# Moving the weight sums of a group behind the low parts beside them, and the weight casts behind the bank copies, in a two-layer decoder trunk

## The chip, the cores and the metric

The kernel runs on one core of a Trainium2 chip. The metric is device time of one execution in microseconds (us), the median of several executions. The engines are named as in the profile: PE is TensorE (PEld its weight loads), DVE is VectorE, ACT is ScalarE, POOL is GpSimd, SP is SyncE, which issues most DMA transfers.

## The reference

Two layers over 256 tokens with a model width of 2048, batch 1, everything in float32:

```
h = x
layer 0: hn = rms_norm(h);  proj = hn @ w_in   (2048 x 6144, split x, y, q, f, v, g)
         RG-LRU on x, y and HGRN2 on q, f, v, g;  h += concat(lru, hgrn) @ w_out
         h += square(relu(rms_norm(h) @ w1)) @ w2      (2048 x 8192, 8192 x 2048)
layer 1: hn = rms_norm(h);  q, k, v = hn @ w_qkv;  rotary, dilated window attention (16 heads)
         h += attn @ w_o
         h += square(relu(rms_norm(h) @ w1)) @ w2
out = rms_norm(h)
```

Nearly all the work is products of a 256-row activation with large weights that are each used once.

## The kernel before

**Precision in two parts.** A weight tile of 128 x 2048 floats (1 MB) is brought in and split: ACT casts it to a high part, tile `hi`, and DVE subtracts that from the tile and leaves the low part, tile `lo`. Activations are held in two parts too (`bufa`, `bufb`, `formx`, `formh`). A product is then three products: high by high, low by high, and high by low. `Weights.split` issues the cast and the subtraction. There are three buffers each for the incoming tile (`raw`), for `hi` and for `lo`.

**Groups with seven products instead of eight.** Most products (half of `w_out` and `w_o`, all of `w_qkv`, `w1` and `w2`) run in groups. A group treats two blocks of 128 tokens, two interleaved halves of the depth and two column blocks of 512 as a 2 x 2 by 2 x 2 product and does it with seven products of blocks. `blocks` runs one group, `combine` prepares its weights. There are 40 groups in the program, 32 of them in the two MLPs. In the table `ORDERS` a group's steps are

```
a  t1  d  t2  n  c  n  t3  n  t4  n        (a few groups exchange the last two, or the two plain tiles)
```

`a`, `d`, `c` are weight tiles as they come. `t1` uses a sum of two tiles, `s = a + t1` (DVE, the first sum). `t2` uses `s + c` (DVE, the second sum, `add("s", "s", "c")`). `t3` uses a tile to which a POOL-issued DMA adds another tile on its way in (tile `t`), and `t4` uses `s` after such an accumulating DMA. The steps `n` are plain tiles used for both token blocks and take twice the time on PE.

**Banks.** The group accumulates in four PSUM banks, `alpha`, `beta`, `gamma`, `delta`. Step `a` fills `beta`, and a copy on ACT carries it into `gamma` before step `d` adds to `gamma`. Step `t1` fills `alpha`, and a second copy carries it into `delta`, which the `n` steps need. `t2` goes on in `beta`. The copies are issued by `seed`. In the profile the first copy reads `COPY p<-pd`, `p<-po` or `p<-pt`, the second `COPY p<-p`. Step `d` on PE reads `p<-hi,bufa` or `p<-hi,bufb`, step `t1` is `p<-hi,formx` or `formh` and `p<-lo,...`, step `t2` the same with `pd`, `po` or `pt` on the left.

**What sets the order.** All instructions of one engine run in the order of its queue. That order is made when the program is built: a scheduler picks the next ready instruction by priority, where weights (`stream`) come 150 places and evacuations and seeds (`urgent`) 400 places early. `after(ins, names)` adds an edge that only orders two instructions. Weight tiles are fetched two steps ahead: `unit` of step `a` fetches `d` (and with it `c` and the second sum), `unit` of `t1` fetches `t2`, and so on.

In the kernel before, the second sum is issued ahead of the split of `d`, except in two groups: the one of `w2` that starts at tile 56 (`LATE_SUM`) and the one of `w1` that starts at tile 64. The first sum has an edge to the low part of the tile before it in one group of `w_qkv` only.

Of the kernel before, what the change touches and what calls it, by code (L numbers as in the profile page):

```python
# [41 lines left out]
def trunk_kernel(ctx, tc, head, x, xtok, xback, cols, tab, masks, pos, fin, w_in, w_gate, w_out, w_qkv, w_o, w1, w2, out):  # L42
# [15 lines left out]
    class InOrder:  # L58
        on = False

        def __init__(self, engine):
            self.engine, self.last = engine, []
# [12 lines left out]
    V, A, T = InOrder(nc.vector), InOrder(nc.scalar), nc.tensor  # L75
# [27 lines left out]
    made = {}  # L103
    loads, casts = [], []
# [26 lines left out]
                    plan2(src, layer * 64 + q * 16 + 4 * n)  # L131
    at = [0, 0]

    class Weights:
        def __init__(self, raw, step=2048):
            self.raw = raw
            self.hi = whi.tile([P, 2048], F32R, name="hi")
            self.lo = wlo.tile([P, 2048], F32R, name="lo")
            for at in range(0, 2048, step) if step else ():
                self.split(at, step)  # L140

        def split(self, at, n, w=None):
            h, l = self.part(at, n)
            if w is None:
                w = self.raw[:, at:at + n]
            else:
                h, l = (t.rearrange("p (k c) -> p k c", c=512) for t in (h, l))
            casts[:] = [after(A.copy(h, w), [])]

            def low():  # L150
                i = V.tensor_tensor(l, w, h.bitcast(F32), OP.subtract)
                self.ins = getattr(i, "ins", i)
            if InOrder.on and ticks:
                lows.append(low)
            else:
                low()
# [20 lines left out]
    def combine(u, src, i, what, i0):  # L177
        def load(name, j, home=wraw):
            held[name] = home.tile([P, 2048], F32, name="raw" if home is wraw else name)
            nc.sync.dma_start(held[name], src[j])  # L180

        def add(to, x, y):
            return V.tensor_tensor(held[to], held[x], held[y], OP.add)

        if what == "a":
            load("t1", i0 + 4, both)
            load("a", i)
            held["s"] = both.tile([P, 2048], F32, name="s")
            i = add("s", "a", "t1")
            if src is w_qkv and i0 == 8:  # L190
                after(i, [made[u - 1].ins.name])
        elif what in ("n", "d"):
            load(what, i)
        def make(step=2048):
            made[u] = Weights(held[{"t1": "s", "t2": "s", "t3": "t1", "t4": "s"}.get(what, what)], step)

        ahead = units[u + 1][2:3] if u + 1 < len(units) else ()
        if ahead == ("t2",):
            load("c", i0 + 5)
            nc.gpsimd.dma_start(held["t1"], src[i0 + 5], accum_op=OP.add)  # L200
            if (src is w2 and i0 == LATE_SUM) or (src is w1 and i0 == 64):
                make()
                after(add("s", "s", "c"), [made[u].ins.name])
                return
            add("s", "s", "c")
        make()
        if what == "c":
            nc.gpsimd.dma_start(held["s"], src[i0 + 1], accum_op=OP.add)
# [49 lines left out]
    def mm(*args, **kw):  # L258
        chain[:] = [after(T.matmul(*args, **kw), chain)]  # L259
# [6 lines left out]
    def flush(due=None):  # L266
        todo = later[:due]
        del later[:due]
        for f in todo:
            f()  # L270
# [8 lines left out]
    def after(ins, names):  # L279
        ins = getattr(ins, "ins", ins)  # L280
        for n in names:
            tc.add_manual_dep(ins, n, NOSYNC, reason="order on one engine")
        return ins.name
# [384 lines left out]
    def lru_in(n, half):  # L668
        b0 = 4 * n + 2 * half
        p = turned("po", [done[f"x{n}"]] * 2, (2 * half, 2 * half + 1), back=True)  # L670
        for i in range(2):
            b = b0 + i
            A.activation(xc[:, b], p[:, i], AF.Identity, bias=col("conv_b", b), scale=col("conv_w", 24 + b))
            for t in range(3):
                V.scalar_tensor_tensor(xc[:, b, 3 - t:], p[:, i, :S - 3 + t], col("conv_w", 8 * t + b),
                                       xc[:, b, 3 - t:], op0=OP.mult, op1=OP.add)
            yield
        split_to(bufb[:, b0:b0 + 2], xc[:, b0:b0 + 2])
        yield
# [36 lines left out]
    def lru_gelu(n):  # L716
        y = done[f"y{n}"]
        q = outs[f"y{n}"] = vgs.tile([P, 2, 512], F32, name="tk", bufs=7)
        for j in range(2):
            A.activation(q[:, j], y[:, j], AF.Square, scale=math.sqrt(0.044715))  # L720
            V.scalar_tensor_tensor(q[:, j], q[:, j], 1.0, y[:, j], op0=OP.add, op1=OP.mult)
            lut(q[:, j], q[:, j], AF.Sigmoid, scale=2.0 * math.sqrt(2.0 / math.pi))
            V.tensor_tensor(y[:, j], y[:, j], q[:, j], OP.mult)
            yield
# [9 lines left out]
    def reload():  # L734
        for j in range(2):
# [3 lines left out]
                 c=[lru_in(0, 0), lru_in(0, 1), lru_in(1, 0), lru_in(1, 1),  # L739
                    lru_gelu(0), lru_out(0, 0), lru_out(0, 1), lru_gelu(1), lru_out(1, 0), lru_out(1, 1)],  # L740
# [91 lines left out]
    def blocks(src, i0, n0, mov, forms, events, final):  # L832
        plain = lambda j, k: (mov[:, k, j * P:j * P + P], mov[:, k, S + j * P:S + j * P + P])
        form = lambda f, k: (forms[:, k, 0, f * P:f * P + P], forms[:, k, 1, f * P:f * P + P])
        side = {"a": lambda i: plain(0, 2 * i), "d": lambda i: plain(0, 2 * i + 1), "t4": lambda i: plain(1, 2 * i + 1),
                "t1": lambda i: form(3, i), "t2": lambda i: form(0, i), "t3": lambda i: form(1, i),
                "c": lambda i: form(2, i)}
        alpha, delta, gamma = (pmm.tile([P, 512], F32, name="p") for _ in range(3))
        beta = psc.tile([P, 512], F32, name=("pd" if i0 % 16 else "pt") if src is w_qkv else "po" if n0 else "pd", bufs=1)
        bank = {"a": beta, "t1": alpha, "t2": beta, "c": alpha, "t3": beta, "d": gamma, "t4": beta}  # L840
        sums = {(0, 0): gamma, (0, 1): beta, (1, 0): alpha, (1, 1): delta}
        opened = []

        def times(bank, w, get, at=0, m=512, out_=None):
            out_ = bank if out_ is None else out_
            parts = [(i, k, 0) for i in range(4) for k in range(2)] + [(i, 0, 1) for i in range(4)]
            for n, (i, k, low) in enumerate(parts):
                mm(out_, get(i)[k], w.part(i * 512 + at, m)[low], start=not any(b is bank for b in opened),
                   stop=n == 11, skip_group_check=True)
                opened.append(bank)  # L850

        def seed(to, bank):
            with urgent():
                A.copy(to, bank)
            opened.append(to)

        plains, did = [0, 0], []
        for what, u in order_of(src, i0 + 4 * n0):
            w = unit(src, None if u is None else i0 + 4 * n0 + u)
            due = len(later)  # L860
            did.append(what)
            if what == "t4" and plains[0] == 2:
                times(beta, w, side[what], 0, S, beta[:, :S])
                final(0, 1, beta)
                rest = psc.tile([P, 512], F32, name="pt", bufs=1)
                times(rest, w, side[what], S, S, rest[:, :S])
                events["rest"](rest[:, :S])
            elif what != "n":
                times(bank[what], w, side[what])
                if what == "a":  # L870
                    seed(gamma, beta)
                elif what == "t1":
                    seed(delta, alpha)
                elif what in events:
                    events[what](bank[what])
                if what == "t2":
                    flush(due)
            else:
                n, g = divmod(u, 4)
                plains[n] += 1  # L880
                for j in range(2):
                    times(sums[n, j], w, lambda i, j=j, g=g: plain(j, 4 * g + i))
                    if plains[n] == 2 and (n, j, "t4" in did) != (0, 1, False):
                        final(n, j, sums[n, j])
                flush(due)
            turn_some()
            for f in steps.pop(0) if steps else ():
                f()
# [283 lines left out]
    with urgent():  # L1172
        for j in range(2):
# [13 lines left out]
            h = tmp.tile([P, 2], F32, name="nr2", bufs=2)[:, :1]  # L1187
# [38 lines left out]


LAST = 2
LATE_SUM = 56
PRIO = 150  # L1230
URGENT = 400
ORDER = "v0 x0 x1 q0 G0 f0 q1 f1 G1 v1 g0 y0 g1 y1"
# [116 lines left out]
```

## Time and profile before

| | |
|---|---|
| median of 3 executions | 2151.09 us (2147.95, 2151.09, 2156.37) |
| profiled execution | 2153.47 us, span of its instructions 2151.7 us |
| mean granted TensorE clock | 0.996 |
| PE busy | 2116.8 us, 98% of the span, 9712 matmuls |
| DVE busy | 1725.2 us, 80% |
| ACT busy | 1359.9 us, 63% |
| DMA | 500.15 MB, mean 232 GB/s |

The time is that of the executions, the span is the stretch between first and last instruction in the one profiled execution, 1.8 us shorter. PE is the engine that is nearly always at work, so the table is read as follows: any gap on PE is time, and work on the other engines matters only where PE waits for it. In a timeline row the columns are start and duration in us, engine, line, operation, output and inputs, shape and count; brackets at the end give the idle time of that engine just before the row, and what released it. Almost all rows stand on L68 (a helper that issues for ACT and DVE) or L259 (the helper of matmuls), so tiles tell them apart.

### The profile page before, as it was taken

The numbers are of one execution on the slowest core, as the hardware profiler recorded it, in microseconds if no ns is written. First come the engines' busy times: TensorE is split into PE (matmuls) and PEld (weight loads), VectorE is DVE, ScalarE is ACT, GpSimd is POOL, SyncE is SP. The second block draws the span as 40 slices with busy tenths as digits, with TensorE's granted clock in tenths as the row PEclk, the third lists the DMA queues.
The fourth block names the chain that finished last, engine by engine and source line by source line (L and its number), as shares of the span: only waits on it lengthen the run. The fifth ranks groups of instructions, "written<-read, shape, count | busy, mean of one in ns | idle before, by whom it ended". The sixth has DMA issues, their size and how long they took to land.

```text
span 2151.7 us, 24879 instructions
## 1 busy us (share of the span) xinstructions
PE 2116.8 (98%) x9712; PEld 1753.8 (82%) x9712; DVE 1725.2 (80%) x1640; ACT 1359.9 (63%) x1438; POOL 72.3 (3%) x89
## 2 busy tenths in 40 slices
PE   9999999999999999999999999999999999999998
PEld 8888888878878888878888888887888888788787
DVE  7686969887778888788887788788878877877787
ACT  7577556665566566576666666566755755655664
POOL 0000000000000000000000000000000000000000
PEclk9999999999999999999999999999999999999999
DMA  8444457777877787778777767477877787778775
GB/s 341 176 176 157 170 218 237 237 223 236 266 251 217 249 260 253 248 228 268 234 242 239 232 225 231 160 215 235 247 271 233 240 253 262 217 235 266 249 246 157
DMA packets 70453, 500.15 MB, mean 232 GB/s; under 512 B 7872, under 2 KB 8128, under 8 KB 10560
## 3 DMA queue, kind: packets, MB, share of 16 engines
q1 hardware_dynamic: 58176, 413.29, 49.1%
q0 software_dynamic: 11872, 84.94, 21.6%
q8 instruction: 76, 1.25, 0.2%
q10 hardware_dynamic: 288, 0.34, 0.0%
q14 instruction: 41, 0.34, 0.0%
HBM read 496.44 MB, written 2.10 MB: 232 GB/s over the span
## 4 chain that ended last, share of the span: by engine, by line
PE 78%; DMA 8%; DVE 6%; ACT 4%; issue 3%; DVEq 0%; ACTq 0%
PE p L259 54%; PE po L259 9%; PE pd L259 8%; DMA raw<-in_w 7%; DVE s L68 3%; ACT hi L68 3%; DVE lo L68 3%; PE pt L259 3%; PE pl L262 2%; PE pl L259 1%; ACT p L68 1%; DMA t<-in_w 0%; DMA t<-in_w_qkv 0%; DVE xall L68 0%; DVE y L68 0%
## 5 line engine op out<-in xcount | busy, mean ns | idle before, releaser
L68 DVE TENSOR_TENSOR lo<-raw,hi 128x2048 fp32r<-128x2048 f32 (+1 forms) x364 | 785.8, 2170 | 115.9 <-ACT hi L68 114.9
L68 ACT CAST hi<-raw 128x2048 fp32r<-128x2048 f32 (+1 forms) x364 | 659.3, 1817 | 284.6 <-PE pd L259 79.7
L259 PE MATMUL p<-hi,bufa 128*128 128x512 f32 x2000 | 511.8, 398 | 19.2 <-ACT p L68 19.2
L259 PEld LDWEIGHTS p<-hi,bufa 128*128 128x128 f32 x2000 | 374.7, 190 | 101.1 <-ACT p L68 25.7
L68 DVE TENSOR_TENSOR lo<-s,hi 128x2048 fp32r<-128x2048 f32 x120 | 274.8, 2290 | 65.8 <-ACT hi L68 63.9
L259 PE MATMUL p<-hi,bufb 128*128 128x512 f32 x1264 | 319.9, 392 | 5.8 <-ACT p L68 5.8
L68 ACT CAST hi<-s 128x2048 fp32r<-128x2048 f32 x120 | 229.3, 1911 | 150.3 <-PE p L259 78.4
L259 PEld LDWEIGHTS p<-hi,bufb 128*128 128x128 f32 x1264 | 235.2, 188 | 57.0 <-ACT p L68 9.0
L259 PE MATMUL p<-lo,bufa 128*128 128x512 f32 x1000 | 269.8, 390 | 0.0
L259 PEld LDWEIGHTS p<-lo,bufa 128*128 128x128 f32 x1000 | 188.0, 188 | 40.0 <-DVE lo L68 0.3
L259 PE MATMUL p<-lo,bufb 128*128 128x512 f32 x632 | 172.9, 389 | 0.0
L68 DVE TENSOR_TENSOR s<-s,raw 128x2048 f32<-128x2048 f32 x40 | 91.6, 2291 | 82.5 <-DMA raw<-in_w 75.5
L68 DVE TENSOR_TENSOR lo<-t,hi 128x2048 fp32r<-128x2048 f32 x40 | 91.6, 2291 | 63.2 <-ACT hi L68 63.2
L259 PEld LDWEIGHTS p<-lo,bufb 128*128 128x128 f32 x632 | 118.7, 188 | 24.8
L68 ACT CAST hi<-t 128x2048 fp32r<-128x2048 f32 x40 | 76.5, 1913 | 91.7 <-PE p L259 85.8
L68 DVE TENSOR_TENSOR s<-raw,t 128x2048 f32<-128x2048 f32 x40 | 91.3, 2283 | 0.4 <-DMA raw<-in_w_o 0.4
L259 PE MATMUL pd<-hi,bufa 128*128 128x512 f32 x352 | 88.5, 393 | 0.6 <-DVE y L68 0.5
L259 PE MATMUL p<-hi,formx 128*128 128x512 f32 x352 | 87.6, 391 | 0.0
L259 PE MATMUL po<-hi,bufb 128*128 128x512 f32 (+1 forms) x320 | 78.6, 388 | 0.4 <-DVE xall L68 0.4
L68 ACT ACTIVATE y<-y 128x512 f32<-128x512 f32 x96 | 60.6, 631 | 26.1 <-DVE y L68 23.8
L259 PEld LDWEIGHTS pd<-hi,bufa 128*128 128x128 f32 x352 | 65.0, 188 | 14.3 <-DVE y L68 1.4
L259 PEld LDWEIGHTS p<-hi,formx 128*128 128x128 f32 x352 | 65.6, 188 | 13.4
(314 smaller groups left out, 2529.8 us busy)
## 6 DMA issues: line engine op xcount, KB each, us to landing
raw<-in_w SPq DMA_DIRECT2D x224, 1024.0 KB, 8.4
raw<-in_w_in SPq DMA_DIRECT2D x45, 1024.0 KB, 4.8
raw<-in_w_qkv SPq DMA_DIRECT2D x42, 1024.0 KB, 7.8
t<-in_w SPq DMA_DIRECT2D x32, 1024.0 KB, 6.4
t<-in_w POOLq DMA_DIRECT2D x32, 1024.0 KB, 9.3
s<-in_w POOLq DMA_DIRECT2D x32, 1024.0 KB, 9.2
raw<-in_w_out SPq DMA_DIRECT2D x15, 1024.0 KB, 4.8
raw<-in_w_o SPq DMA_DIRECT2D x15, 1024.0 KB, 4.9
```

The source lines that it names most:

```text
L68: i = call(*args, **kw)
L259: chain[:] = [after(T.matmul(*args, **kw), chain)]
L262: chain[:] = [after(T.transpose(out_, in_, ident), chain)]
```

## The change

Three things are done to the order; no arithmetic and no transfer is added or removed.

- The second sum `s + c` is issued behind the split of `d` in every group, with an edge to the low part of `d`.
- The first sum `s = a + t1` gets an edge to the low part of the tile before it, in every group whose preceding tile has one.
- The cast of a weight tile gets an edge to the bank copy that was issued last (`seeds`).

```diff
+    seeds = []
+
     class Weights:
         def __init__(self, raw, step=2048):
-            self.raw = raw
+            self.raw, self.ins = raw, None
...
-            casts[:] = [after(A.copy(h, w), [])]
+            casts[:] = [after(A.copy(h, w), seeds)]
...
             held["s"] = both.tile([P, 2048], F32, name="s")
             i = add("s", "a", "t1")
-            if src is w_qkv and i0 == 8:
+            if u - 1 in made and made[u - 1].ins:
                 after(i, [made[u - 1].ins.name])
...
             nc.gpsimd.dma_start(held["t1"], src[i0 + 5], accum_op=OP.add)
-            if (src is w2 and i0 == LATE_SUM) or (src is w1 and i0 == 64):
-                make()
-                after(add("s", "s", "c"), [made[u].ins.name])
-                return
-            add("s", "s", "c")
+            make()
+            after(add("s", "s", "c"), [made[u].ins.name])
+            return
         make()
...
         def seed(to, bank):
             with urgent():
-                A.copy(to, bank)
+                seeds[:] = [after(A.copy(to, bank), [])]
             opened.append(to)
```

Three places show what that does to the queues. The first is DVE in a group of `w1` in layer 0 (its two sums; `t_4401` is the second operand of its first sum, the `xall` rows are results of the group before it). Lines with - stand in the kernel before, lines with + in the changed one.

```order
 L68 TENSOR_TENSOR lo<-s,hi 128x2048
 L68 SCALAR_TENSOR_TENSOR xall<-po,r2n,xall 128x512
+L68 TENSOR_TENSOR lo<-raw,hi 128x2048
 L68 TENSOR_TENSOR s<-raw,t_4401 128x2048
-L68 TENSOR_TENSOR lo<-raw,hi 128x2048 x2
+L68 TENSOR_TENSOR lo<-raw,hi 128x2048
 L68 TENSOR_TENSOR lo<-s,hi 128x2048
 L68 SCALAR_TENSOR_TENSOR xall<-p,nm_3307,xall 128x512
-L68 TENSOR_TENSOR s<-s,raw 128x2048
 L68 SCALAR_TENSOR_TENSOR xall<-po,nm_3307,xall 128x512
 L68 TENSOR_TENSOR lo<-raw,hi 128x2048
+L68 TENSOR_TENSOR s<-s,raw 128x2048
```

The first sum now has the low part of the preceding tile ahead of it, and the second sum (`s<-s,raw`) has moved behind the low part of `d`.

The second place is ACT in the same group, around its two bank copies (`hi<-s` is the cast for `t2`).

```order
 L68 CAST hi<-s 128x2048
 L68 CAST hi<-raw 128x2048
-L68 CAST hi<-s 128x2048
-L68 COPY p<-pd 128x512
-L68 CAST hi<-raw 128x2048
-L68 COPY p<-p 128x512
-L68 CAST hi<-raw 128x2048 x2
+L68 COPY p<-pd 128x512
+L68 COPY p<-p 128x512
+L68 CAST hi<-s 128x2048
+L68 CAST hi<-raw 128x2048 x3
```

Both copies now stand ahead of the cast for `t2` and of the one for the plain tile behind it.

The third place is ACT in the group behind that one (`y_...` and `formh` are results of the `w1` group before it on their way to `w2`).

```order
-L68 CAST hi<-raw 128x2048
+L68 CAST formh<-y_4613 128x2x2x128
+L68 CAST hi<-raw 128x2048
+L68 CAST formh<-y_4532 128x2x2x128
 L68 ACTIVATE y_4740<-pd 128x512
-L68 CAST formh<-y_4613 128x2x2x128
+L68 COPY p<-po 128x512
 L68 ACTIVATE y_4740<-y_4740 128x512
-L68 CAST hi<-s 128x2048
-L68 COPY p<-po 128x512
-L68 CAST formh<-y_4532 128x2x2x128
```

Here the two `formh` casts have moved ahead as well, to both sides of the cast of `d`, and the copy stands between two activations.

The pattern of the second place, both copies and then the cast for `t2`, holds in 37 of the 40 groups. Two of them had it before, the ones whose second sum was already late. In the three attention groups of `w_qkv` that are left the cast for `t2` stays between the two copies. The order on PE does not change; on POOL the transfers keep their order, except that two loads of the final gains pass one accumulating transfer near the end.

More of the change, by code (lines that the diff above doesn't have):

```diff
@@ L1228 @@
 LAST = 2
-LATE_SUM = 56
 PRIO = 150
```

## The prediction

> **What bounds the kernel now.** I read the busy shares of the page first, then the waits of PE, then the timeline around the largest of them.
>
> ```profile
> PE 2116.8 (98%) x9712; PEld 1753.8 (82%) x9712; DVE 1725.2 (80%) x1640; ACT 1359.9 (63%) x1438; POOL 72.3 (3%) x89
> ...
> PE p L259 <- ACT p L68: 24.9, 23, 3.0
> ...
> DVE s L68 <- DMA raw<-in_w: 75.5, 29, 4.0
> ```
>
> PE is at work for 98% of the span, so only its gaps can be won or lost. Nearly all that the profile names of them is one wait, 24.9 us in 23 pieces: step `d`, which adds to a bank that ACT has to fill by the first copy. The third row is what stands behind it: DVE waits 29 times for the tile `c` that its second sum needs. One `w1` group of layer 0 shows how the two hang together:
>
> ```profile
> 569.68 1.91 ACT L68 CAST hi<-raw 128x2048 fp32r<-128x2048 f32 x1 [3.48 <-PE po L259]
> ...
> 571.55 2.29 DVE L68 TENSOR_TENSOR s<-s,raw 128x2048 f32<-128x2048 f32 x1 [2.36 <-DMA raw<-in_w]
> ...
> 573.11 1.98 PE L259 MATMUL p<-hi,formx 128*128 128x512 f32 x8
> ...
> 573.95 1.92 ACT L68 CAST hi<-s 128x2048 fp32r<-128x2048 f32 x1 [2.36 <-DVE s L68]
> 574.42 2.28 DVE L68 TENSOR_TENSOR lo<-raw,hi 128x2048 fp32r<-128x2048 f32 x1
> 574.92 1.07 PE L259 MATMUL p<-lo,formx 128*128 128x512 f32 x4
> 575.77 0.58 ACT L68 COPY p<-pd 128x512 f32<-128x512 f32 x1
> ...
> 576.40 2.11 PE L259 MATMUL p<-hi,bufa 128*128 128x512 f32 x8 [0.42 <-ACT p L68]
> ...
> 581.07 1.07 PE L259 MATMUL pd<-lo,formx 128*128 128x512 f32 x4
> ```
>
> Step `a` ends when `t1` starts, at 573.11, so the copy could run from about 573.3. But ACT is held by the cast for `t2` ahead of it in the queue, that cast waited 2.36 us for the sum, and the sum waited 2.36 us for its tile. The copy comes at 575.77, and `d` at 576.40.
>
> The next group is one of the four worst:
>
> ```profile
> 614.93 2.29 DVE L68 TENSOR_TENSOR s<-s,raw 128x2048 f32<-128x2048 f32 x1 [3.36 <-DMA raw<-in_w]
> ...
> 617.59 0.62 ACT L68 CAST formh<-y 128x512 fp32r<-128x512 f32 x1 [2.75 <-DVE y L68]
> 617.67 1.07 PE L259 MATMUL p<-lo,formx 128*128 128x512 f32 x4
> 618.65 1.88 ACT L68 CAST hi<-s 128x2048 fp32r<-128x2048 f32 x1
> 620.44 0.57 ACT L68 COPY p<-po 128x512 f32<-128x512 f32 x1
> 621.07 3.58 PE L259 MATMUL p<-hi,bufa 128*128 128x512 f32 x8 [2.32 <-ACT p L68]
> 627.34 1.07 PE L259 MATMUL po<-lo,formx 128*128 128x512 f32 x4
> ```
>
> Here the late sum also holds small DVE work on `y`, that holds a `formh` cast on ACT, and the copy comes behind all of it. And the eight matmuls after the wait take 3.58 us.
>
> **The unit of account.** I measure a group from the start of the low matmuls of `t1` to the start of the low matmuls of `t2`. A group without a wait gives the length:
>
> ```profile
> 664.49 1.08 PE L259 MATMUL p<-lo,formh 128*128 128x512 f32 x4
> 665.40 2.01 PE L259 MATMUL p<-hi,bufb 128*128 128x512 f32 x8
> 669.97 1.07 PE L259 MATMUL pd<-lo,formh 128*128 128x512 f32 x4
> ```
>
> That is 5.48 us (669.97 less 664.49). The short-wait group has 581.07 less 574.92, 6.15, and loses 0.67: the row shows 0.42 of it, the other 0.25 is the drain ahead of a gap and the refill behind it. The worse group has 9.67 and loses 4.19: 2.32 waiting, 1.60 in slow matmuls (3.58 less 1.98), 0.27 the same drain and refill.
>
> **What goes.** Both copies now stand ahead of the cast for `t2`, and that cast no longer needs to end before `d`. The first copy then runs 0.2 us after `a`, in time for `d`. So the 24.9 us go, with them 23 x 0.25 = 5.8 us of drain and refill, and the slow matmuls of the four long waits:
>
> ```profile
> 447.36 3.62 PE L259 MATMUL p<-hi,bufa 128*128 128x512 f32 x8 [2.44 <-ACT p L68]
> ...
> 1506.49 2.12 PE L259 MATMUL p<-hi,bufa 128*128 128x512 f32 x8 [1.79 <-ACT p L68]
> ...
> 1847.26 3.43 PE L259 MATMUL p<-hi,bufa 128*128 128x512 f32 x8 [2.58 <-ACT p L68]
> ...
> 2021.08 3.54 PE L259 MATMUL p<-hi,bufa 128*128 128x512 f32 x8 [2.98 <-ACT p L68]
> ...
> 621.00:625.00 4.00, 3.94 (x10) 3.15 (x11) 4.00 (x4) 3.16 (x5) 0.86 (x1) 0.57 0.72 262
> ```
>
> 3.62, 3.58, 3.43 and 3.54 against 1.98 are 6.3 us. The last row, of the stretches by window, gives a granted clock of 0.57 behind the wait of 2.32; behind 1.79 the eight took 2.12, so the clock stayed. Together 24.9 + 5.8 + 6.3 = 37.0 us go.
>
> [...]
>
> **What comes.** The cast for `t2` now starts only when the second copy is done, and that copy waits for `t1` to end. The kernel before has this order in two groups, and the one at 1047 shows its length:
>
> ```profile
> 1045.83 2.29 DVE L68 TENSOR_TENSOR s<-s,raw 128x2048 f32<-128x2048 f32 x1
> ...
> 1046.71 1.07 PE L259 MATMUL p<-lo,formh 128*128 128x512 f32 x4
> ...
> 1047.82 0.57 ACT L68 COPY p<-p 128x512 f32<-128x512 f32 x1 [1.25 <-PE p L259]
> ...
> 1048.31 1.92 ACT L68 CAST hi<-s 128x2048 fp32r<-128x2048 f32 x1
> ...
> 1050.26 2.29 DVE L68 TENSOR_TENSOR lo<-s,hi 128x2048 fp32r<-128x2048 f32 x1 [0.94 <-ACT hi L68]
> ...
> 1053.11 1.07 PE L259 MATMUL po<-lo,formh 128*128 128x512 f32 x4
> ```
>
> From 1046.71 the copy, the cast and the subtraction end at 1052.55, 5.84 us later. There it cost nothing, because transposes on PE held `t2` until 1053.11. In a group without transposes at that place the low matmuls of `t2` are due after 5.48. They will wait 5.84 + 0.06 (the step from an end on ACT to PE, as from 575.77 + 0.58 to 576.40, rounded up) less 5.48, that is 0.42 us, plus a refill of 0.13 (2.11 against 1.98): 0.55. The high part is ready at 1050.23, 3.52 after `t1`'s low matmuls, and `t2` starts at 3.63 (0.91 + 2.72), so it does not wait.
>
> Of the 40 groups nine are spared: the two with this order already, three attention groups whose cast stays between the copies, and four that have transposes around there (the groups at the start of `w_out`'s half, of `w_o`'s, of the first `w1` and of `w_qkv`). 31 x 0.55 = 17.0 us come, including nine groups that wait for nothing today. Net: 37.0 less 17.0, **20.0 us**.
>
> **The rest at nothing, and what covers it.** The second sum moves behind `d`'s low part: in the 570 group that part can run from 571.59 (end of the cast) to 573.9 and the sum to 576.2, before the cast for `t2` can start (by the 1047 group the second copy ends 1.7 us after 574.92, at 576.6). 0.4 us of cover. `d`'s own low part comes 2.8 us earlier than today, and its buffer with it. The first sum moves behind a low part, 2.29 us later, and the accumulating POOL transfer behind it too:
>
> ```profile
> 560.99 0.87 POOL L200 DMA_DIRECT2D t<-in_w  x1 [22.43 <-DVE s L68]
> ...
> 579.19 0.86 POOL L208 DMA_DIRECT2D s<-in_w  x1 [17.34 <-DVE lo L68]
> ...
> 586.71 1.91 ACT L68 CAST hi<-t 128x2048 fp32r<-128x2048 f32 x1 [2.73 <-PE p L259]
> ...
> t<-in_w POOLq DMA_DIRECT2D x32, 1024.0 KB, 9.3
> ```
>
> Issued at 563.3 it lands near 573.5, 13 us before its cast; the second one moves from 579.2 to about 580.8, with some 6 us to spare. The SP queue keeps its order; its tiles come free no later, apart from the plain tile's (about 2 us), which is needed over 8 us later. The plain tile behind `t2` is cast right behind `t2`: its low part ends 8.1 us (5.84 + 2.29) after the start of `t1`'s low matmuls, which I call the mark, and is needed at 8.75 (5.90, 0.13 of refill, 0.91 for the low matmuls of `t2`, then 1.81 for its own high ones): 0.6 us of cover, and part of the upper end.
>
> **Bounds.** A new wait costs at least the 0.42 alone without refill, 13 us in all, and if half of the groups find some other PE work there, 9 us: a gain of 28. With 0.3 us more in every group, for a sum or a plain tile that comes a little late, 26 us come: a gain of 11. I take 0.55, the row closest to it.
>
> **Rivals.**
>
> *The sum comes too late (slower).* The second sum has lost its place ahead of `d`'s low part, and every casting step behind it hangs on it. Cover is 0.4 us; beyond that each 0.1 us costs 3.1 us over 31 groups. At 0.4 + 20.0/31 = 1.05 us late the gain is used up, at 1.4 us the kernel is slower by 0.5%. That needs tile `c` to land after the moment when `d`'s low part is done (573.9 in the 570 group) by 1.05 us. For it: DVE waits for `c` in 29 groups. Against it: the sum starts at 571.55 there, and in the latest group,
>
> ```profile
> 2014.94 2.29 DVE L68 TENSOR_TENSOR s<-s,raw 128x2048 f32<-128x2048 f32 x1 [4.02 <-DMA raw<-in_w]
> ...
> 2017.03 1.07 PE L259 MATMUL p<-lo,formx 128*128 128x512 f32 x4
> ```
>
> still 2.1 us ahead of the mark (the break-even lies just behind it). If it came 2 us too late everywhere: 62 less 12 of cover comes, and 2153.47 + 50 - 20 = 2183 us. Chance 0.07.
>
> *The long waits stay (no change).* In the four groups with the long waits ACT has two `formh` casts and an activation to do around `d`'s cast. If these still come late there, 10.3 of waiting, 6.3 of slow clock and 1.0 stay, less their new waits of 2.2: the gain is 20.0 - 15.4 = 4.6, and 2146.5 on the median. Against it: the `y` work hung on the late sum (2.75 us in the row at 617.59), and the order has it ahead of the sum now. Chance 0.1.
>
> *The slow matmuls don't hang on the waits.* Then 6.3 us stay, 2137.4. Against: four of four, behind the four longest waits and nowhere else. Chance 0.05. That the order does not do what it says is excluded by the rows of the order.
>
> **How the numbers follow.** The profiled execution took 2153.47 us, 2.4 above the median of 2151.09; less 20.0 it is 2133.5, and from the median 2131. That is the forecast, chance 0.78 with its own bounds (2123 to 2140). The range reaches from 2121 (the gain of 28 and the executions' spread of some us) to 2143, which takes in the slow-matmul case and part of the no-change case. Within 0.5%, 10.8 us, is about what a measurement of this kernel can't tell from no change. Faster by more than that 0.83 (forecast and the third rival), same 0.10, slower 0.07.
>
> **What would show it.** In the changed profile the wait of PE at `p` for ACT falls from 24.9 us to under 3; a new wait of `pd`/`po` on DVE `lo`, about 30 times 0.3 to 0.5 us, takes its place; no eight matmuls over 3 us; `COPY p<-p` directly ahead of `CAST hi<-s`; DVE's wait for `c` falls well below 75.5. The prediction is wrong if PE waits for `hi` at `t2`, or if the new waits average over 1 us.

## The result and the profile after

| | before | after |
|---|---|---|
| median of 12 runs each | 2152.05 us (2147.95 to 2158.07) | 2158.91 us (2156.40 to 2166.04) |
| profiled execution / span | 2153.47 / 2151.7 us | 2160.15 / 2158.4 us |
| mean granted TensorE clock | 0.996 | 0.997 |

The ratio is 1.0034, with a 95% interval of 1.0022 to 1.0046. The changed kernel is slower by a third of a per cent. It lies within the 0.5% that I called "same", but not in the range 2121 to 2143, and 28 us above the forecast.

The waits of PE in the changed kernel (columns: engine, bank and line, what was waited for, us in total, times, longest):

```profile
PE pd L259 <- DVE y L68: 9.8, 8, 2.0
PE po L259 <- DVE y L68: 3.7, 8, 1.3
PE po L259 <- DVE xall L68: 3.2, 5, 1.1
PE pd L259 <- DVE lo L68: 3.1, 15, 0.2
PE po L259 <- DVE lo L68: 3.1, 15, 0.2
PE pd L259 <- DVE xall L68: 2.3, 2, 1.9
...
PE pt L259 <- DVE lo L68: 0.2, 1, 0.2
```

The wait for the first copy is gone entirely (24.9 us before), and so is DVE's for tile `c` (75.5 us). The three rows for `lo` are the wait that the prediction added, 31 of them. The four rows for `y` and `xall`, 19.0 us in 23 pieces, are in no step of the prediction. `y` and `xall` are what DVE writes when it clears a bank; PE waits to put the next products into that bank.

What leads to such a wait is seen in one `w1` group of layer 0. First the changed kernel, from the low matmuls of `t1` on:

```profile
746.16 1.07 PE L259 MATMUL p<-lo,formx 128*128 128x512 f32 x4
...
747.07 1.98 PE L259 MATMUL p<-hi,bufa 128*128 128x512 f32 x8
...
747.26 0.57 ACT L68 COPY p<-p 128x512 f32<-128x512 f32 x1 [2.15 <-PE p L259]
747.75 1.91 ACT L68 CAST hi<-s 128x2048 fp32r<-128x2048 f32 x1
749.69 2.29 DVE L68 TENSOR_TENSOR lo<-s,hi 128x2048 fp32r<-128x2048 f32 x1 [2.29 <-ACT hi L68]
751.90 6.69 DVE L68 TENSOR_TENSOR lo<-raw,hi 128x2048 fp32r<-128x2048 f32 x3
752.04 1.19 PE L259 MATMUL pd<-lo,formx 128*128 128x512 f32 x4 [0.21 <-DVE lo L68]
...
753.07 1.99 PE L259 MATMUL p<-hi,bufa 128*128 128x512 f32 x8
...
754.21 0.33 SPq L182 DMA_DIRECT2D raw<-in_w  x1
...
763.94 1.91 ACT L68 CAST hi<-raw 128x2048 fp32r<-128x2048 f32 x1 [4.21 <-DMA raw<-in_w]
765.88 2.29 DVE L68 TENSOR_TENSOR lo<-raw,hi 128x2048 fp32r<-128x2048 f32 x1 [3.83 <-ACT hi L68]
768.09 0.68 DVE L68 TENSOR_TENSOR y<-p,y 128x512 f32<-128x512 f32 x1
...
769.35 1.89 ACT L68 CAST hi<-s 128x2048 fp32r<-128x2048 f32 x1
771.27 2.29 DVE L68 TENSOR_TENSOR lo<-s,hi 128x2048 fp32r<-128x2048 f32 x1 [2.50 <-ACT hi L68]
773.48 0.68 DVE L68 TENSOR_TENSOR y<-y,pd 128x512 f32<-128x512 f32 x1
774.21 2.99 PE L259 MATMUL pd<-hi,bufa 128*128 128x512 f32 x8 [1.93 <-DVE y L68]
```

And the same places of the timeline before:

```profile
753.92 4.91 SPq L180 DMA_DIRECT2D raw<-in_w  x3
...
762.37 1.92 ACT L68 CAST hi<-raw 128x2048 fp32r<-128x2048 f32 x1 [0.96 <-DMA raw<-in_w]
...
771.92 0.68 DVE L68 TENSOR_TENSOR y<-y,pd 128x512 f32<-128x512 f32 x1
...
773.81 1.98 PE L259 MATMUL pd<-hi,bufa 128*128 128x512 f32 x8
```

Step `d` begins at 747.07 without a wait; up to here everything is as forecast, and so is the low part of `t2`, for which PE waits 0.21 us at 752.04. Behind that stands the low part of the plain tile, from 751.90. It ends at 754.19, and at 754.21 SP issues the next load. By its timing it goes into the buffer that this tile has just left; the run with the buffer early, below, bears this out. Its cast waits 4.21 us for it. All that follows stands in order in the queues of DVE and ACT behind this cast and its low part: `y<-p,y`, an activation that isn't shown, the cast and low part for `t4`, and at the end `y<-y,pd`, which empties the bank. PE has waited for that bank for 1.93 us when it comes free at 774.16. Before, the same cast waited 0.96 us, and `y<-y,pd` was done 1.2 us ahead of PE.

### The profile page after: what moved, and what is told of

It is laid out like the page before. It is cut to its first block, busy times and chain, and to the rows that moved or that the text cites. A ratio compares the mean times of both kernels' runs of the same rounds, so it can differ in the third digit from the quotient of the medians.

```text
span 2158.4 us, 24813 instructions
## 1 busy us (share of the span) xinstructions
PE 2124.3 (98%) x9712; PEld 1747.3 (81%) x9712; DVE 1723.0 (80%) x1640; ACT 1355.4 (63%) x1438; POOL 72.3 (3%) x89
## 4 chain that ended last, share of the span: by engine, by line
PE 79%; DVE 8%; DMA 5%; ACT 4%; issue 3%; DVEq 0%; ACTq 0%
PE p L259 49%; PE pd L259 12%; PE po L259 11%; DVE lo L68 6%; ACT hi L68 4%; DMA raw<-in_w 4%; PE pt L259 3%; PE pl L262 2%; PE pl L259 1%; DVE y L68 1%; DVE xall L68 1%; DMA raw<-in_w_o 0%; DMA t<-in_w 0%; DMA raw<-in_w_out 0%; DVE formh L68 0%
## 5 line engine op out<-in xcount | busy, mean ns | idle before, releaser
L68 DVE TENSOR_TENSOR lo<-raw,hi 128x2048 fp32r<-128x2048 f32 (+1 forms) x364 | 783.5, 2169 | 204.2 <-ACT hi L68 197.6
L68 ACT CAST hi<-raw 128x2048 fp32r<-128x2048 f32 (+1 forms) x364 | 651.8, 1817 | 297.2 <-DMA raw<-in_w 89.6
L259 PE MATMUL p<-hi,bufa 128*128 128x512 f32 x2000 | 504.2, 393 | 0.0
```

The source lines that it names most:

```text
L68: i = call(*args, **kw)
```

## The experiments

Theory L, for late load, was carried into them: the plain tile's late low part, the load behind it and the queue behind the load make the waits for `y` and `xall`. Against it stood rivals, named in each expectation. In the diffs `...` stands for what is left out. All were timed in 5 rounds against the kernel before, whose median in them was 2152.95 us (first four) and 2153.01 us (last four).

### The casts alone

```diff
+    seeds = []
...
-            casts[:] = [after(A.copy(h, w), [])]
+            casts[:] = [after(A.copy(h, w), seeds)]
...
-                A.copy(to, bank)
+                seeds[:] = [after(A.copy(to, bank), [])]
```

> Only the casts are put behind the copies (both sums stand where they stood before). By the order the cast for `t2` then stands between the two copies. Theory L (late load: in the changed kernel `t2`'s low part comes about 2 us later, the plain tile's low part behind it too, so its buffer and the load into it, and the casts and bank-clearing subtractions behind that load's cast make PE wait for `y` and `xall`): here neither low part is late, so PE's 24.9 us at `p` for ACT go, with their drain and slow matmuls 37 us, no wait of PE for `lo` comes, and those for `y` and `xall` stay under 5 us: about 2152 - 37 = 2115 us, up to 2125 where some loads come late. Rival P (the loads set the pace: what PE wins at `d` it waits for later, whatever the order): waits for `y` and `xall` of 20 us and more, 2145 to 2155 us.

Measured: 2134.17 us, ratio 0.9915 (0.9903 to 0.9928). Both theories missed: 18.8 us are won, half of the 37. The waits:

```profile
DVE s L68 <- DMA raw<-in_w: 89.5, 29, 4.7
...
PE p L261 <- ACT p L68: 4.9, 5, 1.3
PE pd L261 <- DVE y L68: 2.3, 5, 0.8
```

Tile `c` is as late as ever (89.5 us against 75.5), since nothing here brings it sooner. The copies mostly escape it, but what stands behind the sum still comes late in some groups. P falls too, since half of what was won at `d` was kept, and the waits for `y` and `xall` are 5.7 us, not 20. The 19.6 us by which this run stays above the one with the first sum alone (below) are waits and busy time of PE: its list adds up to 14.0 us against 1.8 there, and PE is busy for 2110.5 us against 2103.0.

### The second sum alone

```diff
-            if (src is w2 and i0 == LATE_SUM) or (src is w1 and i0 == 64):
-                make()
-                after(add("s", "s", "c"), [made[u].ins.name])
-                return
-            add("s", "s", "c")
+            make()
+            after(add("s", "s", "c"), [made[u].ins.name])
+            return
```

> Only the second sum is put behind `d`'s low part, in all groups; the first sum and the casts are as before. The order then has both copies ahead of the cast for `t2`, as in the changed kernel, in all but three groups. Theory L: all of the change's waits are there (`lo` 0.44 us in some 30 groups, `y` and `xall` about 22 us): 2155 to 2161 us. Rival F (the first sum, standing later in DVE's queue, holds the work on `y` behind it): the waits for `y` and `xall` are gone, and the time is what was forecast, about 2132 us.

Measured: 2159.04 us, ratio 1.0035 (1.0022 to 1.0048), the time of the whole change and within theory L's range. So this part brings the loss by itself, and the first sum's place does not make the waits for `y`, so rival F falls:

```profile
PE pd L257 <- DVE y L68: 9.4, 8, 2.2
PE po L257 <- DVE y L68: 5.8, 8, 2.0
```

### The first sum alone

```diff
-            self.raw = raw
+            self.raw, self.ins = raw, None
...
-            if src is w_qkv and i0 == 8:
+            if u - 1 in made and made[u - 1].ins:
                 after(i, [made[u - 1].ins.name])
```

> Only the first sum is put behind the low part beside it. Theory L: nothing on PE hangs on it, 2150 to 2154 us, no wait of PE for `y`. Rival F: the waits for `y` and `xall`, 15 to 22 us, come here without the rest: 2165 to 2175 us.

Measured: 2114.54 us, ratio 0.9823 (0.9810 to 0.9835). Both theories missed: the part that I had costed at nothing wins 38.4 us alone. PE waits for nearly nothing:

```profile
PE po L324 <- DVE e L68: 1.1, 1, 1.1
PE pd L259 <- DVE y L68: 0.5, 1, 0.5
```

The next group of the same product shows why. First the timeline before, from the first sum to step `d`:

```profile
772.52 2.28 DVE L68 TENSOR_TENSOR s<-raw,t 128x2048 f32<-128x2048 f32 x1
774.72 2.28 DVE L68 TENSOR_TENSOR lo<-raw,hi 128x2048 fp32r<-128x2048 f32 x1
...
777.03 0.33 SPq L180 DMA_DIRECT2D raw<-in_w  x1
...
785.86 2.29 DVE L68 TENSOR_TENSOR s<-s,raw 128x2048 f32<-128x2048 f32 x1 [1.85 <-DMA raw<-in_w]
...
792.01 2.11 PE L259 MATMUL p<-hi,bufa 128*128 128x512 f32 x8 [0.83 <-ACT p L68]
```

Then with the first sum moved alone:

```profile
759.53 2.29 DVE L68 TENSOR_TENSOR lo<-raw,hi 128x2048 fp32r<-128x2048 f32 x1
761.74 2.28 DVE L68 TENSOR_TENSOR s<-raw,t 128x2048 f32<-128x2048 f32 x1
...
761.85 0.33 SPq L180 DMA_DIRECT2D raw<-in_w  x1
...
771.00 2.28 DVE L68 TENSOR_TENSOR s<-s,raw 128x2048 f32<-128x2048 f32 x1
...
778.09 1.98 PE L259 MATMUL p<-hi,bufa 128*128 128x512 f32 x8
```

Before, the load of `c` starts 4.51 us behind the start of the first of the two operations (777.03 less 772.52), 0.03 us after the end of the low part. Exchanged, it starts after 2.32 us. The sum moves back, and what it moves behind moves forward: the last plain tile of the group before leaves its buffer 2.2 us sooner, and `c` is the next tile to go there. `c` then is in time for the second sum, and every wait for the first copy goes. This is theory B of the later runs. Its rival T: the accumulating transfer into `t1` starts later and leaves the DMA engines to `c`. The load of `c` did take less time too, as the section on the hardware shows.

### The changed kernel with a short low part

Of the low part of the plain tile behind `t2` only 512 of 2048 columns are computed.

```diff
...
+            cut = self.cut or None
...
-                i = V.tensor_tensor(l, w, h.bitcast(F32), OP.subtract)
+                i = V.tensor_tensor(l[:, :cut], w[:, :cut], h[:, :cut].bitcast(F32), OP.subtract)
...
+                              512 if what == "n" and units[u - 1][2:3] == ("t2",) else None)
...
-                mm(out_, get(i)[k], w.part(i * 512 + at, m)[low], start
+                mm(out_, get(i)[k], w.part((0 if low and w.cut else i * 512) + at, m)[low], start
```

> The changed kernel, but of the low part of the first plain tile behind `t2` only the first 512 of 2048 columns are computed (PE multiplies these four times, so its work is the same in shape and count): DVE is done with that tile about 1.7 us earlier and its buffer is free about as early behind `t1` as in the kernel before. Theory L: the load into that buffer is issued about 5.4 us after `t1` ends instead of 7.1, the waits of PE for `y` and `xall` fall from 22.7 us to under 6, the waits for `lo` (13 us) stay: 2159 - 17 to - 25, that is 2134 to 2142 us. Rivals P and F: PE waits as much as in the changed kernel, 2155 to 2160 us.

Measured: 2130.95 us, ratio 0.9899 (0.9885 to 0.9913), 28 us below the changed kernel, 3 us more than the upper end of what theory L had. The expectation's 22.7 us of waits for `y` and `xall` are 19.0 by the list of the changed kernel. No such wait is left here. This speaks for L, but DVE also has 1.6 us less to do in each group (its low parts of `raw` tiles add up to 721.3 us against 783.5, over 40 groups).

### Only the buffer earlier, in both kernels

To part the buffer from DVE's time, the low part was cut in two pieces of the same total length, of which only the first reads the raw tile. The second leaves zeros in place of the low part. The order on every engine stays. In the kernel before it is the plain tile ahead of the first sum, in the changed kernel the one behind `t2`.

```diff
...
-                i = V.tensor_tensor(l, w, h.bitcast(F32), OP.subtract)
+                if not self.early:
+                    i = V.tensor_tensor(l, w, h.bitcast(F32), OP.subtract)
+                else:
+                    m, f = self.early, h.bitcast(F32)
+                    V.tensor_tensor(l[:, :m], w[:, :m], f[:, :m], OP.subtract)
+                    i = V.tensor_tensor(l[:, m:], f[:, m:], f[:, m:], OP.subtract)
...
+                              512 if what == "n" and u + 1 < len(units) and units[u + 1][2:3] == ("a",) else 0)
```

(In the changed kernel the last condition is `units[u - 1][2:3] == ("t2",)`.)

> The kernel before, its order on every engine unchanged, but the low part of the last plain tile of each group in two pieces: 512 columns from the raw tile, and the other 1536 as the high part less itself, which doesn't read the raw tile and leaves zeros there. DVE's time for it stays near 2.3 us; the raw buffer is free about 1.7 us earlier. Theory B (the first sum's move alone gains 38 us because the low part ahead of it frees its buffer 2.3 us earlier and tile `c` is loaded into that buffer): `c` comes 1.7 us earlier, of the 23 waits of PE for the first copy those of up to 1.7 us go, about 20 of 24.9 us with drain and slow matmuls: 2118 to 2127 us. Rival T (the move gains because the accumulating transfer into `t1` starts 2.3 us later and leaves the DMA engines to `c`'s load): that transfer is where it was, 2150 to 2155 us.

Measured: 2114.01 us, ratio 0.9824 (0.9811 to 0.9838), 4 us below theory B's range: every wait for the first copy went, and not only those of up to 1.7 us. The timeline at the place shown above:

```profile
759.25 2.28 DVE L68 TENSOR_TENSOR s<-raw,t 128x2048 f32<-128x2048 f32 x1
761.45 0.69 DVE L68 TENSOR_TENSOR lo<-raw,hi 128x512 fp32r<-128x512 f32 x1
762.05 1.75 DVE L68 TENSOR_TENSOR lo<-hi 128x1536 fp32r<-128x1536 f32 x1
762.07 0.86 POOL L207 DMA_DIRECT2D t<-in_w  x1 [23.93 <-DVE s L68]
...
762.17 0.33 SPq L186 DMA_DIRECT2D raw<-in_w  x1
```

The first sum is where it was and the accumulating transfer follows it as before. Only the load of `c` comes sooner, 2.92 us behind the start of the sum instead of 4.51, and with the order on every engine unchanged this wins all that the moved sum won. Theory B is shown. T falls as it was put, since the transfer is issued no later. What T says of the DMA engines does not fall with it: `c` is now issued 0.10 us behind the transfer instead of 1.70 (777.03 less 775.33, the transfer's row there) and lands 5.9 us after its issue instead of 8.7. So a load issued 1.6 us sooner landed 4.4 us sooner (2.92 + 5.9 against 4.51 + 8.7 from the start of the sum), more than the 1.7 us that the expectation counted with.

> The changed kernel, its order on every engine unchanged, but the low part of the first plain tile behind `t2` in the same two pieces (1536 columns as the high part less itself): DVE is done with it as late as in the changed kernel, the raw buffer alone is free 1.7 us earlier. Theory L (the late load into that buffer makes the waits for `y` and `xall`): they go as in the run with the short low part, 2129 to 2136 us. Rival D (there DVE itself was relieved by 1.7 us a group, and that took the waits away): 2153 to 2160 us, the waits for `y` and `xall` near 20 us.

Measured: 2130.73 us, ratio 0.9900 (0.9886 to 0.9913), within theory L's range. All waits of PE for `y` and `xall` are gone, those for `lo` are the same:

```profile
PE pd L266 <- DVE lo L68: 3.2, 15, 0.2
PE po L266 <- DVE lo L68: 3.2, 15, 0.2
```

DVE is no shorter at that tile than in the changed kernel (0.68 + 1.75 us against 2.29 in the group shown), so D falls: the buffer's release, through the loads that wait for it, is what costs 28.2 us (2158.91 less 2130.73).

### The parts two by two

The first sum and the casts together, without the second sum:

> The first sum behind the low part beside it and the casts behind the copies; the second sum where it was before. Theory B: `c` is early, so nothing is left for the casts to win, and the cast for `t2` between the copies costs nothing: 2112 to 2117 us. Rival O (casts behind copies cost something of their own, as the casts alone stayed 20 us above the first sum alone): 2120 to 2135 us.

Measured: 2114.56 us, ratio 0.9822 (0.9809 to 0.9836), as theory B had it; O falls. The casts behind the copies cost nothing and bring nothing once `c` is early.

Both sums, without the edge of the casts:

> Both sums moved, the casts without their edge. Theory L: the late second sum alone decides, the first sum's gain is lost in it, because the cast for `t2` can't start before the second copy: 2156 to 2161 us, with `lo` 6.4, `y` and `xall` about 20 us in PE's waits. Rival S (the gain of the first sum and the loss of the second add up): 2152 - 38 + 6, that is 2120 us.

Measured: 2158.56 us, ratio 1.0034 (1.0021 to 1.0046), as theory L had it; S falls. The gain of the first sum and the loss of the second do not add up, since both end the same wait: with the second sum behind `d`'s low part the copies stand ahead of the cast anyway, so an early `c` has nothing left to win.

## Why the prediction was wrong, step by step

- *What goes, 37.0 us:* right in size. The runs in which these waits go and no other comes win 38.4 us (first sum alone) and 39.0 us (the buffer early in the kernel before). The changed kernel lost this wait as forecast.
- *What comes, 31 x 0.55 = 17.0 us:* right, though the sign named for it was not. From the low matmuls of `t1` to those of `t2` the changed group takes 5.88 us (752.04 less 746.16), 0.40 more than 5.48, and the next matmuls start 1.03 us later (753.07) instead of 0.91: 0.52 us a group, against 0.55. Over all groups it is 16.2 us, the changed kernel with the early buffer less the first sum with the casts (2130.73 less 2114.56). The profile's row shows only 0.2 us of each as a wait, 6.4 us in 31 pieces, not the 0.3 to 0.5 that I expected there.
- *"its tiles come free no later, apart from the plain tile's (about 2 us), which is needed over 8 us later":* this is the step that failed. I saw the delay and named a cover for it without following it through. In the group above, before, the load was issued at 753.92 and cast at 762.37, 8.45 us later; but it took 8.3 us from issue to landing, so the 8 us were nearly all the load's own time. The wait at the load's other end tells the same, and the profile before had that row:

```profile
ACT hi L68 <- DMA raw<-in_w: 33.5, 25, 2.7
```

  ACT already waited 25 times for a load ahead of a cast. There was no cover there, and the 1.2 us that PE still had at `y<-y,pd` were all. In the changed kernel the row reads

```profile
ACT hi L68 <- DMA raw<-in_w: 89.6, 31, 4.4
```

  and the delay cost 28.2 us instead of nothing.
- *The first sum moves behind a low part, at nothing:* wrong as well, though not in the sum of the change. I followed the sum backwards and its transfer, and not the low part that moved forwards, and so missed that this one edge removes the same 37 us at no cost.
- *The sum:* -37.0 + 17.0 was forecast; -38.4 + 16.2 + 28.2 = +6.0 by the runs, +6.9 measured. The three are steps along one chain of runs, so their adding up says no more than that the first sum alone and with the casts takes the same time; each step by itself is what the runs show.
- *Rivals:* the sum did not come too late (PE has no wait for `hi` in the list), and the long waits did not stay. Of the third, the slow matmuls went with their waits (none over 2.3 us with the first sum alone), but new ones came behind the new waits. The way to a slower kernel that did occur was none of the three.
- *What would show it:* the copy's wait, the order of copy and cast and the wait for `c` came as listed, and the new wait for `lo` in its number but not in its size. "No eight matmuls over 3 us" did not (one took 3.35), and the two signs of failure that I named were not the one that came.

The best order found is the first sum moved alone, 2114.54 us. It is faster than both kernels: 38.4 us below the one before in the same rounds, and 2.1% below the 2158.91 us of the changed one.

## What to carry to other kernels

When two instructions change places, follow both, and from each the buffer it frees, the load that waits for that buffer, and the wait at that load's far end; where a row there already shows a wait for DMA, as here (33.5 us in 25 pieces), a delay has no cover. Look too at what else is being transferred when the load starts. Where several edits end the same wait, their gains don't add, while a cost that one of them brings stays, so each is worth costing and trying alone. Here the one that only released a buffer 2 us sooner was worth more than the three together.

## What the runs showed of the hardware

A load can lose more than it was delayed. In the changed kernel the load issued at 754.21 held its cast until 763.94, 9.7 us. With the buffer early the cast of that load no longer waits for it:

```profile
740.49 1.98 PE L266 MATMUL p<-hi,bufa 128*128 128x512 f32 x8
...
746.04 0.33 SPq L188 DMA_DIRECT2D raw<-in_w  x1
...
753.98 1.92 ACT L68 CAST hi<-raw 128x2048 fp32r<-128x2048 f32 x1 [0.76 <-PE p L266]
```

Counted from the start of step `d` (747.07 and 740.49), the load is issued 1.59 us later in the changed kernel (7.14 against 5.55), and by the times from issue to landing it lands 4.2 us later (16.74 against 12.55). Those times go with the place of the load beside the accumulating transfer that POOL issues near it. In the two groups shown:

| kernel, load | issue of the load, from that of the transfer | load, issue to landing | transfer, issue to landing |
|---|---|---|---|
| before, `c` | 1.70 us behind | 8.7 us | 9.2 us |
| before, buffer early, `c` | 0.10 us behind | 5.9 us | 12.2 us |
| first sum alone, `c` | 2.70 us ahead | 4.7 us | 8.9 us |
| before, behind the plain tile | 1.93 us behind | 8.3 us | 8.6 us |
| changed, behind the plain tile | 1.93 us behind | 9.6 us | 9.2 us |
| changed, buffer early, the same | 0.34 us behind | 7.0 us | 12.9 us |

The 32 groups of the MLPs show the same. The load of `c` takes 8.7 to 10.1 us in 30 of them in the kernel before, 5.6 to 7.5 in 30 with the buffer early, and 4.7 to 5.8 in all with the first sum alone. The load behind the plain tile takes 7.8 to 10.2 us in the kernel before, 8.4 to 10.2 us in the changed kernel and 5.9 to 8.9 with the buffer early. Issued 0.10 and 0.34 us behind the transfer instead of 1.70 and 1.93, the load took 5.9 and 7.0 us instead of 8.7 and 9.6, and the transfer 12.2 and 12.9 instead of 9.2 in both; the medians of that transfer over its 32 issues say the same, 12.2 and 12.6 us with the buffer early against 9.3 and 9.2. That the two slow each other is my reading of these times. No run moved the transfer alone, so how much of the 39.0 and 28.2 us comes from this and how much from the earlier issue is open. Between the kernel before and the changed one the place is the same in the group shown, 1.93 us behind (over the 32 groups 1.63 to 2.61 us before and 1.64 to 1.94 in the changed kernel), so there this did not make the changed kernel slower; it may be why a buffer given back early wins so much.

The slow clock came after shorter waits than before, and not by length alone. In the kernel before, the shortest wait with a slow clock behind it was that of 2.32 us (granted clock 0.57), and behind 1.79 us the clock was 1.00. In the changed kernel it was 0.62 behind a wait of 1.93 us and 1.00 behind one of 1.92 us, and eight matmuls behind a wait of 1.99 us took 3.35 us. The timeline and, below it, the stretches by window (us, then busy time of PE, PEld, DVE, ACT and POOL, granted clock, DMA share, GB/s):

```profile
600.57 3.35 PE L259 MATMUL pd<-hi,bufa 128*128 128x512 f32 x8 [1.99 <-DVE y L68]
```

```profile
600.50:604.50 4.00, 3.93 (x10) 3.13 (x11) 4.00 (x3) 1.80 (x3) 0.00 (x0) 0.58 0.20 33
```

With the second sum alone eight matmuls behind a wait of the same length took 2.14 us, at full clock; the same two views:

```profile
1709.65 2.14 PE L257 MATMUL po<-hi,bufa 128*128 128x512 f32 x8 [1.99 <-DVE y L68]
```

```profile
1709.60:1713.60 4.00, 3.95 (x21) 3.37 (x22) 4.00 (x2) 3.25 (x4) 0.88 (x1) 1.00 0.00 0
```

So a wait of the same length was followed by the slow clock once (0.58) and by the full clock once (1.00). What decides besides the length, no run shows.
